# A pooled store of two tiles, sent as two transfers of the even and of the odd partitions

**Chip and metric.** One core of a Trainium2 chip. The time is device microseconds of one execution, as a median of several; before the change 3103.71 us over four runs (3103.39 to 3103.87). The experiments ran in three batches on other chips of the same kind, each with the kernel before beside it (medians 3103.55 to 3103.66 us).

## The reference

Average pooling, window 2 by 2 and step 2, over 32 x 128 planes of 256 by 256 float32:

```python
x = np.random.randn(32, 128, 256, 256).astype(np.float32)   # kernel_size 2, stride 2
for i in range(h_out):
    for j in range(w_out):
        window = x[:, :, 2*i:2*i + 2, 2*j:2*j + 2]
        output[:, :, i, j] = np.mean(window, axis=(2, 3))
```

1073.7 MB are read and 268.4 MB written, each byte once, and there is next to nothing to compute.

## The kernel before

A tile holds 32 pairs of input rows on each of 128 partitions: 64 KB a partition, 8 MB in all. Two input tiles and two result buffers exist. SyncE loads the even partitions of each tile and ScalarE's queue the odd ones, so each load is 64 partitions with a step of two. VectorE adds the two rows and then neighbouring columns, ScalarE multiplies by 0.25, and the results of two tiles lie side by side in one buffer of 32 KB a partition. GpSimd stores that buffer when both are scaled; it then waits for the store before this one and tells VectorE that that one's buffer is free.

```python
xp = xv[0:last].rearrange("(k o p t g) f -> t o k p g f", o=2, t=2, p=P // 2, g=TILE)
op = ov[0:last].rearrange("(k o p g) f -> k p o (g f)", o=2, p=P // 2, g=2 * TILE)
# ...
def load(odd, k, b):
    (act if odd else sp).dma_start(out=ins[b][odd::2], in_=xp[b, odd][k]).then_inc(loaded[b], 16)

def sums(it, dst):
    dve.tensor_add(out=it[:, :, 0:w], in0=it[:, :, 0:w], in1=it[:, :, w:]).then_inc(halfway)
    take(dve, halfway)
    dve.tensor_add(out=dst, in0=it[:, :, 0:w:2], in1=it[:, :, 1:w:2]).then_inc(summed)

def tile_sums(t):
    if t % 2 == 0:
        take(dve, emptied[t // 2 % 2])      # the result buffer is free
    take(dve, loaded[t % 2], 32)            # both halves of the tile are there
    sums(ins[t % 2], res[t % 4])
# ...
def store(k, c):
    take(pool, scaled, 2)
    pool.dma_start(out=op[k], in_=both[c].rearrange("p t g f -> p (t g f)")).then_inc(stored[c], 16)

def emptied_by(c, landed):
    pool.wait_ge(stored[c], landed)
    pool.sem_inc(emptied[c])
# ... the GpSimd program:
store(0, 0)
with pool.Fori(0, (pairs - 3) // 2) as i:
    for c in (1, 0):
        store(2 * i + (2 - c), c)
        emptied_by(1 - c, 16 * i + 16)
# ... the last pair's store is SyncE's; one tile and three pieces follow as a tail
```

Of the kernel before, what the change touches and what calls it, by code (L numbers as in the profile page):

```python
# [9 lines left out]
@with_exitstack  # L10
def kernel(
    ctx: ExitStack,
    tc: tile.TileContext,
    x: bass.AP,
    kernel_size: bass.AP,
    stride: bass.AP,
    out: bass.AP,
):
    nc = tc.nc
    P = nc.NUM_PARTITIONS  # L20

    n, c, h, w = x.shape
    k = int(kernel_size)
    s = int(stride)
    h_out = (h - k) // s + 1
    w_out = (w - k) // s + 1
    R = n * c * h_out
    units = R // P if R % P == 0 else 0


    if k == 2 and s == 2 and h % 2 == 0 and w == 256 and units >= 1024 and (units - 1) // 64 % 2 and (units - 1) // 32 % 2:
        _pool_2x2(ctx, tc, x, out, units)
    else:
        _generic_pool(ctx, tc, x, out, k, s, n, c, h, w, h_out, w_out)


TILE = 32


def _pool_2x2(ctx, tc, x, out, units):  # L40
    nc = tc.nc
    P = nc.NUM_PARTITIONS
    f32 = mybir.dt.float32
    w = x.shape[3]
    w_out = w // 2
    sp, act, dve, pool = nc.sync, nc.scalar, nc.vector, nc.gpsimd

    xv = x.rearrange("n c (ho a) w -> (n c ho) (a w)", a=2)
    ov = out.rearrange("n c ho wo -> (n c ho) wo")









    in_pool = ctx.enter_context(tc.tile_pool(name="inp", bufs=2))
    out_pool = ctx.enter_context(tc.tile_pool(name="outp", bufs=2))  # L60
    ins = [in_pool.tile([P, TILE, 2 * w], f32, name="in_tile") for _ in range(2)]
    both = [out_pool.tile([P, 2, TILE, w_out], f32, name="res") for _ in range(2)]
    res = [both[t // 2][:, t % 2] for t in range(4)]

    def sem(name):
        return ctx.enter_context(nc.semaphore(name))

    loaded, free, stored, emptied = [
        [sem(f"{n}{b}") for b in range(2)] for n in ("loaded", "free", "stored", "emptied")
    ]  # L70
    halfway, summed, scaled, held, done, tail = [
        sem(n) for n in ("halfway", "summed", "scaled", "held", "done", "tail")
    ]



    def take(engine, sem, n=1):
        engine.wait_ge(sem, n)
        engine.sem_inc(sem, -n)  # L79

    def block(r0, g):
        rows = slice(r0, r0 + g * P)
        return xv[rows].rearrange("(p g) f -> p g f", p=P), ov[rows].rearrange("(p g) f -> p g f", p=P)

    pairs, rest = divmod(units - TILE - 1, 2 * TILE)
    whole, rest = 2 * pairs + 1, rest + 1
    assert pairs % 2 and pairs >= 5 and rest <= TILE
    last = 2 * pairs * TILE * P
    xp = xv[0:last].rearrange("(k o p t g) f -> t o k p g f", o=2, t=2, p=P // 2, g=TILE)
    op = ov[0:last].rearrange("(k o p g) f -> k p o (g f)", o=2, p=P // 2, g=2 * TILE)  # L90
    parts, a = [], 0
    while a < rest:
        b = rest if rest - a <= 8 else a + (rest - a) // 2
        parts.append((a, b, sem(f"part{len(parts)}")))
        a = b

    def load(odd, k, b):
        (act if odd else sp).dma_start(out=ins[b][odd::2], in_=xp[b, odd][k]).then_inc(loaded[b], 16)

    def load_block(odd, dst, r0, g, landed):  # L100
        (act if odd else sp).dma_start(out=dst[odd::2], in_=block(r0, g)[0][odd::2]).then_inc(landed, 16)

    def load_last(odd):
        for a, b, part in parts:
            load_block(odd, ins[whole % 2][:, a:b], (whole * TILE + a) * P, b - a, part)
# [8 lines that stand above are left out]
            take(dve, emptied[t // 2 % 2])  # L114
        take(dve, loaded[t % 2], 32)
        sums(ins[t % 2], res[t % 4])

    def scale(dst, sem):
        act.mul(out=dst, in_=dst, mul=0.25).then_inc(sem)  # L119

    def next_load(b, *what):

        take(act, summed)
        act.sem_inc(free[b])
        what[0](1, *what[1:])

    def store(k, c):
        take(pool, scaled, 2)
        pool.dma_start(out=op[k], in_=both[c].rearrange("p t g f -> p (t g f)")).then_inc(stored[c], 16)  # L129

    def emptied_by(c, landed):
        pool.wait_ge(stored[c], landed)
        pool.sem_inc(emptied[c])

    with tc.tile_critical():

        for b in range(2):
            load(0, 0, b)
        with sp.Fori(1, pairs) as k:
            for b in range(2):  # L140
                take(sp, free[b])
                load(0, k, b)
        take(sp, free[0])
        load_block(0, ins[0], last, TILE, loaded[0])
        take(sp, free[1])
        load_last(0)
        take(sp, held, 2)
        c = (pairs - 1) % 2
        sp.dma_start(out=op[pairs - 1], in_=both[c].rearrange("p t g f -> p (t g f)")).then_inc(tail, 16)


        for b in range(2):
            dve.sem_inc(emptied[b])
        with dve.Fori(0, whole // 4):
            for t in range(4):
                tile_sums(t)
        for t in range(whole - whole % 4, whole):
            tile_sums(t)
        it = ins[whole % 2]
        dst = ins[(whole + 1) % 2].rearrange("p g (s f) -> p (g s) f", s=4)[:, 0:TILE]  # L160
        for a, b, part in parts:
            take(dve, part, 32)
            sums(it[:, a:b], dst[:, a:b])


        for b in range(2):
            load(1, 0, b)
        with act.Fori(0, (pairs - 1) // 2) as i:
            for c in range(2):
                for b in range(2):  # L170
                    next_load(b, load, 2 * i + (c + 1), b)
                    scale(both[c][:, b], scaled)
        c = (pairs - 1) % 2
        next_load(0, load_block, ins[0], last, TILE, loaded[0])
        scale(both[c][:, 0], held)
        next_load(1, load_last)
        scale(both[c][:, 1], held)
        take(act, summed)
        scale(res[(whole - 1) % 4], done)
        take(act, done)  # L180
        act.dma_start(out=block(last, TILE)[1], in_=res[(whole - 1) % 4]).then_inc(tail, 16)
        for a, b, _ in parts:
            take(act, summed)
            scale(dst[:, a:b], done)
            take(act, done)
            act.dma_start(out=block((whole * TILE + a) * P, b - a)[1], in_=dst[:, a:b]).then_inc(tail, 16)


        store(0, 0)
        with pool.Fori(0, (pairs - 3) // 2) as i:  # L190
            for c in (1, 0):
                store(2 * i + (2 - c), c)
                emptied_by(1 - c, 16 * i + 16)
        store(pairs - 2, 1)
        for c in range(2):
            emptied_by(c, 16 * (pairs - 1) // 2)
        pool.drain()


        take(sp, tail, 16 * (len(parts) + 2))  # L200


def _generic_pool(ctx, tc, x, out, k, s, n, c, h, w, h_out, w_out):
# [92 lines left out]
```

## Time and profile before

| | before |
|---|---|
| median of four runs | 3103.71 us |
| span of the profiled run | 3102.0 us |
| sum of all packet times, per DMA engine | 3102.1 us |
| DMA engine idle up to the last packet, mean of the sixteen | 5.1 us, all of it at the start and the end |
| VectorE idle before the row additions | 1390.8 us |

These are lines of the timeline of the kernel before for VectorE alone (start, duration, engine, line, operation; in brackets the idle time ahead of it and what ended that):

```profile
1515.20 8.69 DVE L108 TENSOR_TENSOR in_tile<-in_tile 128x8192 f32<-128x8192 f32 x1 [10.92 <-DVEq L79]
...
1540.58 8.69 DVE L108 TENSOR_TENSOR in_tile<-in_tile 128x8192 f32<-128x8192 f32 x1 [12.11 <-DVEq L79]
...
1587.73 8.69 DVE L108 TENSOR_TENSOR in_tile<-in_tile 128x8192 f32<-128x8192 f32 x1 [11.95 <-DVEq L79]
```

"DVEq L79" is the line of the helper that waits on any semaphore, so the name of the releaser does not say whether it was the load or the result buffer. The landing times do: the tile's last load semaphore came at 1515.07 for the first of these, the buffer's at 1512.46. VectorE waited for the load, here and at all 62 tiles at which it needs an earlier store to be done.

### The profile page before, as it was taken

The numbers are of one execution on the slowest core, as the hardware profiler recorded it, in microseconds if no ns is written. First come the engines' busy times: TensorE is split into PE (matmuls) and PEld (weight loads), VectorE is DVE, ScalarE is ACT, GpSimd is POOL, SyncE is SP. The second block draws the span as 40 slices with busy tenths as digits, with TensorE's granted clock in tenths as the row PEclk, the third lists the DMA queues.
The fourth block names the chain that finished last, engine by engine and source line by source line (L and its number), as shares of the span: only waits on it lengthen the run. The fifth ranks groups of instructions, "written<-read, shape, count | busy, mean of one in ns | idle before, by whom it ended". The sixth has DMA issues, their size and how long they took to land. (4 is left out here: it accounts for less than half of the span.)

```text
span 3102.0 us, 2728 instructions
## 1 busy us (share of the span) xinstructions
DVE 1679.3 (54%) x260; ACT 503.0 (16%) x161; POOL 38.0 (1%) x66
## 2 busy tenths in 40 slices
DVE  5555555555555555555555555555555555555555
ACT  1111112111111111111111111211112111121111
POOL 0000000000000000000000000000000000000000
DMA  9999999999999999999999999999999999999999
GB/s 419 433 434 437 433 433 428 438 433 432 433 440 428 434 441 433 427 433 439 432 433 438 428 438 431 434 434 432 435 436 433 439 432 433 434 431 434 434 433 406
DMA packets 30448, 1342.20 MB, mean 433 GB/s; under 512 B 5232, under 2 KB 5232, under 8 KB 5488
## 3 DMA queue, kind: packets, MB, share of 16 engines
q10 hardware_dynamic: 10976, 541.07, 40.3%
q1 hardware_dynamic: 10544, 541.07, 40.3%
q0 software_dynamic: 8928, 260.05, 19.4%
HBM read 1073.74 MB, written 268.44 MB: 433 GB/s over the span
## 5 line engine op out<-in xcount | busy, mean ns | idle before, releaser
L108 DVE TENSOR_TENSOR in_tile<-in_tile 128x8192 f32<-128x8192 f32 (+1 forms) x130 | 1112.9, 8561 | 1390.8 <-DVEq L79 1390.8
L119 ACT ACTIVATE res<-res 128x4096 f32<-128x4096 f32 x127 | 459.2, 3616 | 1967.0 <-ACTq L79 1943.3
L110 DVE TENSOR_TENSOR res<-in_tile 128x4096 f32<-128x4096 f32 x127 | 561.9, 4425 | 18.6
L119 ACT ACT_TABLE_LOAD x31 | 39.8, 1283 | 613.0 <-ACTq L79 613.0
L129 POOL DMA_DIRECT2D out_dram<-res x62 | 37.8, 610 | 2971.0 <-POOLq L79 2579.3
L119 ACT ACTIVATE in_tile<-in_tile 128x1024 f32<-128x1024 f32 (+1 forms) x3 | 4.0, 1341 | 7.3 <-ACTq L79 7.3
L110 DVE TENSOR_TENSOR in_tile<-in_tile 128x1024 f32<-128x1024 f32 (+1 forms) x3 | 4.7, 1581 | 0.4
L277 POOL MEMSET const-float32-0.0<- 128x1 f32 x1 | 0.1, 93 | 0.4 <-issue 0.4
L277 POOL MEMSET const-bfloat16-1.0<- 128x1 bf16 x1 | 0.1, 95 | 0.0
L277 POOL MEMSET const-float32-1.0<- 128x1 f32 x1 | 0.1, 93 | 0.0
L277 POOL MEMSET const-uint8-127<- 128x1 uint8 x1 | 0.1, 93 | 0.0
## 6 DMA issues: line engine op xcount, KB each, us to landing
out_dram<-res POOLq DMA_DIRECT2D x62, 4096.0 KB, 49.7
out_dram<-res SPq DMA_DIRECT2D x1, 4096.0 KB, 33.4
in_tile<-in_x_dram ACTq DMA_DIRECT2D x1, 2048.0 KB, 15.3
in_tile<-in_x_dram SPq DMA_DIRECT2D x1, 2048.0 KB, 18.1
in_tile<-in_x_dram ACTq DMA_DIRECT2D x2, 1024.0 KB, 23.0
in_tile<-in_x_dram SPq DMA_DIRECT2D x2, 1024.0 KB, 23.1
out_dram<-res ACTq DMA_DIRECT2D x1, 2048.0 KB, 16.1
in_tile<-in_x_dram ACTq DMA_DIRECT2D x127, 32.4
```

The lines of the kernel that those rows point to most:

```text
L108: dve.tensor_add(out=it[:, :, 0:w], in0=it[:, :, 0:w], in1=it[:, :, w:]).then_inc(halfway)
L110: dve.tensor_add(out=dst, in0=it[:, :, 0:w:2], in1=it[:, :, 1:w:2]).then_inc(summed)
L119: act.mul(out=dst, in_=dst, mul=0.25).then_inc(sem)
L129: pool.dma_start(out=op[k], in_=both[c].rearrange("p t g f -> p (t g f)")).then_inc(stored[c], 16)
L277: nc = _bacc.Bacc("TRN2", target_bir_lowering=False, num_devices=1)
```

## The change

Its intent, as its form suggests: stores in the shape that the loads have, each half going to a contiguous 2 MB of the output. Semaphore counts double.

```diff
-    op = ov[0:last].rearrange("(k o p g) f -> k p o (g f)", o=2, p=P // 2, g=2 * TILE)
+    op = ov[0:last].rearrange("(k o p g) f -> o k p (g f)", o=2, p=P // 2, g=2 * TILE)
...
+    def store_from(engine, k, c, landed):
+        for o in range(2):
+            src = both[c][o::2].rearrange("p t g f -> p (t g f)")
+            engine.dma_start(out=op[o][k], in_=src).then_inc(landed, 16)
+
     def store(k, c):
         take(pool, scaled, 2)
-        pool.dma_start(out=op[k], in_=both[c].rearrange("p t g f -> p (t g f)")).then_inc(stored[c], 16)
+        store_from(pool, k, c, stored[c])
...
-        sp.dma_start(out=op[pairs - 1], in_=both[c].rearrange("p t g f -> p (t g f)")).then_inc(tail, 16)
+        store_from(sp, pairs - 1, c, tail)
...
-                emptied_by(1 - c, 16 * i + 16)
+                emptied_by(1 - c, 32 * i + 32)
...
-            emptied_by(c, 16 * (pairs - 1) // 2)
+            emptied_by(c, 16 * (pairs - 1))
...
-        take(sp, tail, 16 * (len(parts) + 2))
+        take(sp, tail, 16 * (len(parts) + 3))
```

## The prediction

Its sum came to 3103.6 + 0.6 = 3104.2 us, put at 3104.5 for the tail.

> **What bounds the kernel now.** I read the page's busy slices first, then its DMA queues, then the groups and waits, and last a stretch of the timeline and the landing times in the middle of the run. The first two say almost everything:

> ```profile
> span 3102.0 us, 2728 instructions
> ...
> DVE 1679.3 (54%) x260; ACT 503.0 (16%) x161; POOL 38.0 (1%) x66
> ...
> DMA  9999999999999999999999999999999999999999
> ...
> q10 hardware_dynamic: 10976, 541.07, 40.3%
> q1 hardware_dynamic: 10544, 541.07, 40.3%
> q0 software_dynamic: 8928, 260.05, 19.4%
> HBM read 1073.74 MB, written 268.44 MB: 433 GB/s over the span
> ```

> No compute engine is busy for more than 54%, the DMA row shows 9 in all 40 slices, and the three queues' packets fill 40.3 + 40.3 + 19.4 = 100.0% of sixteen engines' span. The transfers bound this kernel; nothing is left over for a wait to occupy. The packet records give the same from below: a 64 KB load packet takes 2418 ns and a 32 KB store packet 1213 ns, nearly all of them to the nanosecond, so 27.1 GB/s for each engine and 433 GB/s for sixteen. The packet times add up to 3102.1 us for each engine. Sixteen packets are in flight at practically every moment; fewer than that for under 4 us in all, at the ends.

> The waits of the compute engines are therefore waits for the transfers, which the timeline shows:

> ```profile
> 1549.41 4.42 DVE L110 TENSOR_TENSOR res<-in_tile 128x4096 f32<-128x4096 f32 x1
> 1554.15 0.50 ACTq L98 DMA_DIRECT2D in_tile<-in_x_dram  x1
> ...
> 1559.07 0.61 POOL L129 DMA_DIRECT2D out_dram<-res  x1 [48.95 <-POOLq L79]
> 1562.52 8.69 DVE L108 TENSOR_TENSOR in_tile<-in_tile 128x8192 f32<-128x8192 f32 x1 [8.68 <-DVEq L79]
> ...
> 1576.13 0.50 ACTq L98 DMA_DIRECT2D in_tile<-in_x_dram  x1
> ...
> 1606.22 0.61 POOL L129 DMA_DIRECT2D out_dram<-res  x1 [46.54 <-POOLq L79]
> ```

> VectorE needs 8.69 + 4.42 = 13.1 us for a tile and idles 8.7 to 12.1 us before each. Two tiles, that is one store, go by in 48.4 us. The load issued at 1554.15 is followed by the landing of the tile before it at 1562.4, so 8 us of the previous load were still queued when the new one came; at the next tile (1576.13 against 1587.6) it was 11 us. The engines' queues have 8 to 11 us in hand before a late load could leave them dry.

> The store is the part to look at:

> ```profile
> out_dram<-res POOLq DMA_DIRECT2D x62, 4096.0 KB, 49.7
> out_dram<-res SPq DMA_DIRECT2D x1, 4096.0 KB, 33.4
> ```

> From issue to landing a store takes 49.7 us (last column), a little more than the period. An engine that takes one packet from each queue in turn spends 2 x 2.418 + 1.213 = 6.05 us on a round; a store is 8 packets on each engine, so 8 x 6.05 = 48.4 us. The store thus lasts as long as the tile pair it belongs to, and its buffer is needed again just after: over the run the store lands a median of 3.2 us before the load that VectorE waits for at the same tile (0.2 to 4.1 us).

> [...]

> **The change part by part.** It removes 63 store transfers of 4 MB over 128 partitions and adds 126 of 2 MB over 64 partitions with a step of two. Bytes and size of packet (32 KB) stay: 128 data packets for a pair of tiles before and after, 8 on each engine, now 4 and 4. What changes:

> Completion packets. A GpSimd store has (8928 - 7936) / 62 = 16 of them, one on each engine, of 9 ns in the packet records. There are 63 more on each engine: 63 x 9 ns = 0.57 us, all of it on the bound resource. This is the only certain cost: +0.6 us, or 0.02%.

> Issues. 62 more on GpSimd of at most 0.61 us, 38 us of an engine that is idle for 99% of the time; the landing of the previous store is acknowledged after this second issue, about 0.6 us later than now when that landing came early. In the timeline that is 1559.26 to perhaps 1560.3 against the load's landing at 1562.4: still before. One more issue on SyncE at the end (0.64 us for the last store) is in front of transfers that wait in a queue anyway. On the path: 0.

> Completion in the middle. [...]If the store queue sat out for it, the other two queues have load packets for 4.8 us in every round, so the engine stays busy. At worst the store misses one turn of 4.8 us; less the 3.2 us of slack, VectorE is 1.6 us late, with 8 to 11 us of loads in hand. On the path: 0, as long as something else is queued.

> Order of the writes. Even partitions write one half of an 8 MB block of the output, odd ones the other. Before, an engine's packets could alternate between the halves, now they go through one and then the other. The packets are at their floor of 1213 ns, so this can't gain; and loads in just this shape are at their floor, so I see nothing to lose.

> Sum: 3103.6 + 0.6 = 3104.2 us. What the tail makes of it can move the end by some us either way, more likely later since there is no idle time to win: I say 3104.5.

> **The rivals.** First, that the store's completion becomes the bound: VectorE waits for the buffer and not for its load. For it: only 3.2 us of slack, and a store as long as its period. Against it: when a store lags, loads took its turn, and the engines are no less busy. For a loss, the loads must run dry: delays above 8 us in every pair. If each of 63 pairs lost 2 us of all engines, it would be 126 us, 3230 us; I give this 1 to 2%.

> Second, that the 64-partition store from GpSimd is spread badly, over eight engines for example. For it: no such GpSimd store is in this trace. Against it: loads with the same 64 partitions have 4 packets on each of sixteen engines. If it were so, eight engines would have 38.7 + 19.4 = 58.1 us of packets in each pair instead of 48.4: 20% longer, some 3700 us. I give it 1%.

> Third, that it gains: contention between packets that the old order causes disappears, or the first half of a store starts its buffer sooner. Against it: the buffer is released only after both halves, packets are at their floor, and what is idle in the whole run is startup and tail, some 10 us. The most it could make is about 3095 us.

> **Range and chances.** The three runs before lie within 0.5 us. The certain term is 0.6 us, the tail's phase may be worth 1 to 3 us, and a small loss by queues running short for moments some us more: 3101 to 3110 holds most of it. Faster by over 2% would need 62 us that the engines do not idle: 0.5%. Slower by over 2% is the first two rivals: 2.5%. The rest, 97%, is within 2%.

> **What would show each step.** Right: GpSimd's queue has 8928 + 62 x 16 = 9920 packets and the share of the three queues still adds up to 100%; SP's queue has 16 more; GpSimd shows 124 store issues and 2048 KB each, with the second of a pair landing about 50 us after its issue and the first about 25; 32 KB packets stay at 1213 ns; VectorE's total idle time before the tile additions stays near 1391 us. Wrong: slices of the DMA row below 9 in the middle, packets of over 1213 ns, a store that lands after the load of the same tile, or VectorE idle for well above 1391 us. A change of the end by more than 10 us in either direction would make the prediction wrong, whatever its cause.

## The result

The changed kernel takes 3104.9 us (four runs, 3104.58 to 3105.97) against 3103.71. The ratio is 1.0005 with a 95% interval of 0.9987 to 1.0022: the same. Executions over 1.5% slower than the fastest of the same kernel are left out of the means. (Ratios here are the mean time of one kernel's fast runs over that of the other's fast runs of the same rounds, so not quite the ratio of the medians quoted.)

From the page of the changed kernel, its head and its DMA queues:

```profile
span 3103.3 us, 2911 instructions
...
DVE 1679.3 (54%) x260; ACT 503.0 (16%) x161; POOL 67.2 (2%) x128
...
q10 hardware_dynamic: 10976, 541.07, 40.3%
q1 hardware_dynamic: 10560, 541.07, 40.2%
q0 software_dynamic: 9920, 260.05, 19.4%
...
out_dram<-res POOLq DMA_DIRECT2D x124, 2048.0 KB, 42.0
out_dram<-res SPq DMA_DIRECT2D x2, 2048.0 KB, 32.4
```

The bytes and shares stand as they were, to 0.1%; GpSimd's queue has 992 more packets and SyncE's 16, which are the completion packets. The 42.0 us to landing is a median over both halves of the stores and the time of neither (see below). VectorE's part has changed, though. Its timeline in the same stretch:

```profile
1517.42 8.69 DVE L108 TENSOR_TENSOR in_tile<-in_tile 128x8192 f32<-128x8192 f32 x1 [13.53 <-DVEq L79]
...
1539.00 8.69 DVE L108 TENSOR_TENSOR in_tile<-in_tile 128x8192 f32<-128x8192 f32 x1 [8.32 <-DVEq L79]
...
1557.50 1.12 POOL L132 DMA_DIRECT2D out_dram<-res  x2 [47.27 <-POOLq L79]
1565.78 8.69 DVE L108 TENSOR_TENSOR in_tile<-in_tile 128x8192 f32<-128x8192 f32 x1 [13.52 <-DVEq L79]
...
1587.39 8.69 DVE L108 TENSOR_TENSOR in_tile<-in_tile 128x8192 f32<-128x8192 f32 x1 [8.34 <-DVEq L79]
```

The first tile of each pair now has 13.5 us of idle time ahead of it and the second 8.3, always. The load for the tile at 1565.78 had landed at 1563.1; the buffer's release came at 1565.54, once the last semaphore of the odd half had arrived at 1565.49. VectorE waits for the result buffer instead of the load, by 2.4 us (1.2 at the last), at 62 of these 62 tiles, where before the buffer was first by a median of 3.2 us. The waits, summed over the run (total us, times, longest), before and after:

```profile
DVE in_tile L108 <- DVEq L79: 1390.8, 127, 23.7
```

```profile
DVE in_tile L108 <- DVEq L79: 1393.3, 127, 23.6
```

So the releaser changed and the sum did not: what VectorE waits longer in one tile it waits less in the next, because the transfers set the pace.

**Where the buffer's slack went.** The packet records tell it when they are put in the order in which one DMA engine works. (The records do not name the engine; each packet was given to the engine that had just come free, which leaves no gaps.) L is a 64 KB load packet of 2.418 us, S a 32 KB store packet of 1.213 us, a dot a completion packet of 9 ns; q0 is GpSimd's queue, q1 and q10 those of SyncE and ScalarE. The changed kernel, one engine, start in us:

```
1529.17 q10:L  1531.59 q0:S  1532.80 q1:L  1535.21 q10:.  1535.22 q0:S
1536.43 q1:.   1536.43 q10:L 1538.85 q0:.  1538.85 q1:L   1541.27 q10:L
1543.68 q0:S   1544.89 q1:L  1547.31 q10:L 1549.72 q0:S
```

Counted in turns: an undivided store has 8 data packets on each engine and 1 completion, 9 turns; the divided one has 4 + 1 + 4 + 1 = 10. The loads of the two tiles have 2 x (4 + 1) = 10 turns on each of their queues. Before, the store had a turn to spare in each pair of tiles, and its landings were spaced irregularly (46.4 to 50.3 us, 5th to 95th percentile). Now it has exactly as many turns as the loads, and runs in lockstep with them: landings every 48.35 to 48.45 us, the odd half 24.2 us after the even one, each time one load packet (2.4 us) behind the load that VectorE wants. In the same window of before the dot at 1557.85 was followed by a round in which q0 had nothing, for the next store had been issued only at 1559.07.

**Where the 1.3 us of span went.** The packet times add up to 3102.80 us per engine in place of 3102.15, which is 0.65: the 63 completions of 9 ns (0.57) and less than 0.1 of scatter. The engines' mean idle time rose from 5.1 to 5.9 us, in the last hundred microseconds: VectorE's last pieces begin 2.4 us later (the last small store is issued at 3092.95 against 3090.51). Of these 2.4, 1.1 are the load of the last even tile landing later (3062.97 against 3061.90), and the rest is its buffer, released 1.3 us after that load where before the buffer was first. The two together, 0.65 + 0.86, exceed the 1.3 by 0.2, because packets overlap by some nanoseconds where one hands over to the next (7.0 us for each engine in all before, 7.2 after).

### The profile page after: what moved, and what is told of

It is laid out like the page before. It is cut to its first block, busy times and chain, and to the rows that moved or that the text cites. A ratio compares the mean times of both kernels' runs of the same rounds, so it can differ in the third digit from the quotient of the medians.

```text
span 3103.3 us, 2911 instructions
## 1 busy us (share of the span) xinstructions
DVE 1679.3 (54%) x260; ACT 503.0 (16%) x161; POOL 67.2 (2%) x128
## 2 busy tenths in 40 slices
DMA  9999999999999999999999999999999999999999
## 3 DMA queue, kind: packets, MB, share of 16 engines
q10 hardware_dynamic: 10976, 541.07, 40.3%
q1 hardware_dynamic: 10560, 541.07, 40.2%
q0 software_dynamic: 9920, 260.05, 19.4%
HBM read 1073.74 MB, written 268.44 MB: 432 GB/s over the span
## 5 line engine op out<-in xcount | busy, mean ns | idle before, releaser
L108 DVE TENSOR_TENSOR in_tile<-in_tile 128x8192 f32<-128x8192 f32 (+1 forms) x130 | 1112.9, 8561 | 1393.3 <-DVEq L79 1393.3
L110 DVE TENSOR_TENSOR res<-in_tile 128x4096 f32<-128x4096 f32 x127 | 562.0, 4425 | 18.6
L132 POOL DMA_DIRECT2D out_dram<-res x124 | 67.0, 540 | 2942.3 <-POOLq L79 2939.5
L110 DVE TENSOR_TENSOR in_tile<-in_tile 128x1024 f32<-128x1024 f32 (+1 forms) x3 | 4.7, 1580 | 0.4
## 6 DMA issues: line engine op xcount, KB each, us to landing
out_dram<-res ACTq DMA_DIRECT2D x1, 2048.0 KB, 14.2
in_tile<-in_x_dram ACTq DMA_DIRECT2D x127, 30.9
```

Of the source, the lines that this page charges most:

```text
L132: engine.dma_start(out=op[o][k], in_=src).then_inc(landed, 16)
```

## The experiments

The theory to test: **turns**. What decides is how many packets, completions included, a store has on each engine, against the 10 of the loads. Rivals: **confirmation** (a divided store costs only one more completion, called a receipt in the expectations, and one more issue; how long it would wait for a receipt no trace shows, and the landing times given for this rival were my guess), and **shape** (64 partitions in place of 128, or which 64, is what delays it). I worked expectations out by stepping through the three queues of one engine packet by packet, with the durations that the profile shows.

### Other partitions, same number of turns

```diff
-            src = both[c][o::2].rearrange("p t g f -> p (t g f)")
+            src = both[c][o * 64:o * 64 + 64].rearrange("p t g f -> p (t g f)")
```

> The changed kernel, but each store divided into partitions 0 to 63 and 64 to 127 in place of even and odd. Theory of turns (every packet, a completion packet of 9 ns too, takes a turn in the round of the three queues; a divided store has 8 + 2 = 10 turns, an undivided one 9, the loads of a pair 10 on each of their queues): nothing depends on which partitions, so 3105 us, store landing 2.4 us after the load of the same tile in every pair.[...]

Four executions took 3114.41, 3115.06, 3206.79 and 3219.96 us. The last two count as slow, at the same granted clock of 1.000; only a fast one was profiled (span 3113.4). In that profile the store lands 2.4 us after the load in every pair, as with even and odd, and in the loop its 32 KB packets take 1213 ns. So turns, not partitions, set the lockstep, and the other choice of partitions cost nothing there. The 10 us lie at the end. SyncE's last store runs there with few loads beside it, and after 3080 us its 32 KB packets take a mean of 2012 ns and up to 3367. Landing times and the last stretch of this kernel:

```profile
out_dram<-res SPq DMA_DIRECT2D x2, 2048.0 KB, 37.1
out_dram<-res ACTq DMA_DIRECT2D x1, 2048.0 KB, 22.7
```

```profile
3080.00:3113.00 33.00, 11.42 (x6) 5.70 (x4) 0.00 (x0) 1.00 0.84 263
```

The last figure of the second fence is GB/s: 263, over a stretch whose DMA engines are busy for 84% of it. In the kernel before the same end ran at 339 over 22 us and was done.

The same kernel with its last store whole again:

```diff
-        store_from(sp, pairs - 1, c, tail)
+        sp.dma_start(out=ow[pairs - 1], in_=both[c].rearrange("p t g f -> p (t g f)")).then_inc(tail, 16)
```

The expectation's first case is cut where marked, for the cause that it named and no run shows. If the 10 us are the tail's, it had 3105 us in the fast executions and no 32 KB packets above 1300 ns at the tail.

> The kernel with halves of adjacent partitions in the loop, but the last store undivided. [...]If they come from the loop: 3114 us again. If executions near 3210 us come again, the loop's stores cause them; if all lie within 2 us, the tail or chance did.

3104.88, 3104.90, 3105.56 and 3118.40 us (median 3105.23), ratio 1.0019 [0.9996, 1.0041]. Three of four are at the changed kernel's time and after 3080 us the 32 KB packets are back at 1213 ns: the 10 us were the tail's. The fourth, 13 us longer, cannot come from a divided last store, for this kernel has none; whether the two near 3210 above have the same cause is not shown. No profile of such an execution was had; what makes them slow stays open. No execution of the kernel with even and odd halves (nine, with the loop-only variant below) showed it.

### More transfers

```diff
-        for o in range(2):
-            src = both[c][o::2].rearrange("p t g f -> p (t g f)")
+        for j in range(4):
+            src = both[c][j::4].rearrange("p t g f -> p (t g f)")
```

> The changed kernel, but each store in four transfers, of every fourth partition. Theory of turns: 8 + 4 = 12 turns against the loads' 10; worked through packet by packet, the store lands about 12 us after the load of the same tile and VectorE waits for the buffer, but the loads in hand just cover it: 3106 us (1.1 us more of completion packets than with two). Theory of confirmation[...]: store landing 4 to 5 us after the load, 3106 us too. The time does not tell them apart, the landing does.

3143.0 us, ratio 1.0126 [1.0109, 1.0143]. Neither expectation had the time. The landing went with turns in kind: the store lands up to 14.2 us after the load, a median of 5.6, but not every time; in other pairs it lands 12 us before. The time divides so: of 38.8 us more span, 1.7 are completion packets, 4.2 idle DMA engines and 33 longer load packets, which my bookkeeping held at 2418 ns. Some 680 of the 15,600 in the loop took over 2660 ns, up to 3911; before it was 17. So there is a price even where the queues do not run empty. That uneven pacing of the loads is the cause is my guess, from one likeness: such lengths are also seen in the first 100 us (in the kernel before, 29 of 592 load packets: 13 at 2 to 3 us, where all engines begin to load at once, and 16 at 66 us). No run separates this cause from others.

```diff
-        for o in range(2):
-            src = both[c][o::2].rearrange("p t g f -> p (t g f)")
+        for j in range(8):
+            src = both[c][j::8].rearrange("p t g f -> p (t g f)")
```

> The changed kernel, but each store in eight transfers, of every eighth partition (one data packet and one completion packet on each engine for each). Theory of turns: 16 turns against 10; the store lands some 23 us after the load, the loads run dry while VectorE waits, the DMA engines idle about 3 us in each pair of tiles, period 51.4 us in place of 48.4: about 3290 us, 6% slower. Theory of confirmation: six more receipts and issues of 0.55 us, hidden by the loads in hand: 3108 us.

3440.89 us, ratio 1.1084 [1.1066, 1.1103]. Confirmation's 3108 is out, but turns' 3290 is also short by 150. The queue lines and VectorE's waits of this kernel:

```profile
q10 hardware_dynamic: 10976, 541.07, 37.3%
q1 hardware_dynamic: 10656, 541.07, 37.2%
q0 software_dynamic: 15872, 260.08, 22.9%
```

```profile
DVE in_tile L108 <- DVEq L79: 1722.7, 96, 34.1
```

The same 260 MB of stores now fill 22.9% of a longer span. Their packets have a mean of 1580 ns and their 90th percentile is 2487, twice the 1213. In the packet order it is seen where the loads have run dry and the store queue has the engines for itself: of the S packets that directly follow another S, half take over 2.0 us (mean 1908 ns), of those that follow a load packet 0.1% (mean 1274). No run shows why they take longer there. Against the packets' usual lengths, GpSimd's stores cost 182 us more and the packets of the other two queues, nearly all loads, 69; idle time of the engines is 89 us more, where the bookkeeping had some 186 (3 us in each of 62 pairs). That a store which is itself slow leaves fewer gaps would explain the difference, but was not tested. So this kernel alone does not prove turns: it mixes them with slow store packets.

### Turns without bytes and without division

```diff
         pool.dma_start(out=op[k], in_=both[c].rearrange("p t g f -> p (t g f)")).then_inc(stored[c], 16)
+        for j in range(3):
+            pool.dma_start(out=scr[0:16, c, j], in_=xv[0:16, 0:128]).then_inc(stored[c], 16)
...
-                emptied_by(1 - c, 16 * i + 16)
+                emptied_by(1 - c, 64 * i + 64)
```

> The kernel before, stores undivided over 128 partitions, but after each store GpSimd issues three tiny loads of 512 B on each of 16 partitions into a scratch tile (24 KB in all, one small packet and one completion packet on each engine each), which count towards the release of the store's buffer. Output stays right. Theory of turns: 8 + 1 + 3 x 2 = 15 turns against 10: the last tiny load lands about 20 us after the load of the same tile, period 51.4 us, about 3290 us, 6% slower, for 0.001 of the bytes. Theory that the shape of the divided store (half the partitions) is what delays it: like before, 3104 us. Theory of confirmation: 3106 us.

3373.71 us, ratio 1.087 [1.0852, 1.0888]: the store whole, 128 partitions, packets of 1213 ns, 1.5 MB more in the whole run, and 270 us longer. Shape and confirmation are both out by far. VectorE's timeline of this kernel, and three stretches of it (busy times of three engines, granted clock, DMA share, GB/s):

```profile
1502.08 8.69 DVE L110 TENSOR_TENSOR in_tile<-in_tile 128x8192 f32<-128x8192 f32 x1 [30.90 <-DVEq L81]
...
1515.26 8.68 DVE L110 TENSOR_TENSOR in_tile<-in_tile 128x8192 f32<-128x8192 f32 x1
...
1538.13 8.69 DVE L110 TENSOR_TENSOR in_tile<-in_tile 128x8192 f32<-128x8192 f32 x1 [9.62 <-DVEq L81]
```

```profile
1490.00:1540.00 50.00, 28.01 (x5) 8.52 (x3) 2.08 (x4) 1.00 0.91 378
1540.00:1590.00 50.00, 24.37 (x4) 7.23 (x2) 2.08 (x4) 1.00 0.97 420
1590.00:1640.00 50.00, 26.15 (x4) 8.52 (x3) 0.81 (x2) 1.00 0.86 365
```

VectorE stands for 30.9 us and then does two tiles at a run, the second with no wait: both input tiles lay there loaded, waiting for a result buffer, and with both full no load could be issued. One engine, its packets put in order as above, had nothing to do between 1510.3 and 1517.1. In every second pair the last semaphore of the buffer comes 19.7 us after the load, as the bookkeeping had it (20); in the others it comes 26 us before. Idle time of the engines is 212 us against 5, which is 207 of the 269 us of span; longer load packets are 55, the added packets some 7.

The same edit with one tiny load in place of three:

```diff
+        for j in range(1):
+            pool.dma_start(out=scr[0:16, c, j], in_=xv[0:16, 0:128]).then_inc(stored[c], 16)
```

> The kernel before with one tiny load after each store, counting towards the release of the buffer. Theory of turns: 8 + 1 + 2 = 11 turns against 10, just over the balance: the buffer comes free 5 to 10 us after the load of the same tile, the loads in hand cover it: 3106 us by bookkeeping, up to 3125 us if pauses of the loads slow their next packets as with four transfers. Theory of confirmation: 3104.5 us and a landing 1 to 2 us later than before, that is still ahead of the load.

3136.9 us, ratio 1.0108 [1.0091, 1.0125], above what I gave for the upper end. One turn too many, 11 against 10, and the buffer comes up to 9.8 us after the load (median 4.5); idle time of the engines is only 9.7 us, load packets are 26 us longer in all. Between the divided store's 10 turns and 11 there is a step, 1 us on one side and 33 on the other.

### Same division of bytes, smaller packets

```diff
-            src = both[c][o::2].rearrange("p t g f -> p (t g f)")
+            src = both[c][:, o].rearrange("p g f -> p (g f)")
```

> The changed kernel with the same number of transfers and bytes in each, but divided by tile in place of partition: all 128 partitions, packets of 16 KB. Theory of turns: 16 + 2 = 18 turns against 10, loads run dry in every second pair as with the three tiny transfers: between 3290 us (from bookkeeping with full-speed packets) and 3450 us (store with 15 turns measured 3374). Theory that two transfers of 2 MB cost what they cost whatever the packets: 3105 us.

3361.51 us, ratio 1.0832 [1.0816, 1.0849]. Two transfers of 2 MB each, as in the change, all 128 partitions, and 8% slower: 16 + 2 turns. The 16 KB packets take 611 ns throughout, so no store packet is slowed; the engines idle for 204 us and the buffer is 23.9 us late in every second pair. Load packets over their usual length are another 49 us.

### Giving the loads more turns

```diff
-        (act if odd else sp).dma_start(out=ins[b][odd::2], in_=xp[b, odd][k]).then_inc(loaded[b], 16)
+        for h in range(2):
+            gs = slice(h * TILE // 2, (h + 1) * TILE // 2)
+            (act if odd else sp).dma_start(out=ins[b][odd::2, gs], in_=xp[b, odd][k][:, gs]).then_inc(loaded[b], 16)
```

The expectation, for slow store packets, gave about 3118 + up to 180 us if those packets stay slow beside loads; the 180 are the 182 us of the run with eight transfers.

> The kernel with eight transfers for each store (3441 us), and now the loads are cut as well: each half load goes as two transfers of 32 KB packets. Theory of turns: the loads of a pair have 20 turns on each queue against 16 of the store, so the store is never late and the DMA engines never idle, although more packets are moved: 3104 + 7 x 63 x 9 ns of store completions + 252 x 9 ns of load completions + 1016 x 8 ns for halved packets = 3118 us, ten per cent faster than with whole loads. Rival: the eight transfers are slow by themselves[...]: stays near 3440 us.[...]

3148.02 us, ratio to before 1.0133 [1.011, 1.0156]. The store still goes as eight transfers; only the loads were chopped finer, and 293 of the 337 us came back: by the traces' sums, 83 are idle time of the engines and 174 store packets that are no longer slowed. This is the strongest of the tests, since more packets and more issues made the kernel faster. The store now lands before the load of the same tile in 61 of 62 pairs, by some 5 to 10 us. The waits of this kernel:

```profile
DVE in_tile L110 <- DVEq L79: 1433.7, 127, 24.8
```

VectorE still waits for the buffer at 53 of the 62 tiles, a median of 0.5 us after the load, because GpSimd passes the release on only after it has issued its next eight transfers:

```profile
1578.83 4.54 POOL L134 DMA_DIRECT2D out_dram<-res  x8 [49.23 <-issue]
1583.22 8.69 DVE L110 TENSOR_TENSOR in_tile<-in_tile 128x8192 f32<-128x8192 f32 x1 [13.21 <-DVEq L79]
```

Here the load had landed at 1578.42, the store some 8 us before that, and the release came at 1582.97. The engines hardly idle all the same (11 us), so landing ahead of the load and being released ahead of it are two things.

The remaining 44 us are 14 of added completions and halved packets, as worked out, 8 of store packets and 27 of load packets over their usual length, and 6 of idle engines, which add up to 55; packets that overlap at their handover take some 5 back, and the profiled execution had 49 us more span. With loads between the stores, the 32 KB store packets are nearly back at their usual length (a mean of 1229 ns, against 1580 before the loads were cut).

### Which part of the change costs its microsecond

Two kernels take the change apart: only SyncE's last store divided, or only the loop's.

```diff
-        sp.dma_start(out=op[pairs - 1], in_=both[c].rearrange("p t g f -> p (t g f)")).then_inc(tail, 16)
+        for o in range(2):
+            sp.dma_start(out=oq[o][pairs - 1], in_=both[c][o::2].rearrange("p t g f -> p (t g f)")).then_inc(tail, 16)
```

> The kernel before with only the last store, the one of SyncE, divided in even and odd partitions. If the changed kernel's 1.2 us come from the loop (0.6 us of completion packets, and a last tile that VectorE starts later because the divided store holds its buffer): 3103.7 us, as before. If they come from the divided last store at the tail: 3104.3 us or more.

3103.61 us (five runs, 3103.58 to 3104.11), ratio 1.0 [0.9987, 1.0014].

The other one is the changed kernel with this, the edit shown above for the adjacent halves:

```diff
-        store_from(sp, pairs - 1, c, tail)
+        sp.dma_start(out=ow[pairs - 1], in_=both[c].rearrange("p t g f -> p (t g f)")).then_inc(tail, 16)
```

> The changed kernel with the last store undivided. If the 1.2 us come from the loop: 3104.9 us, as with the whole change, and the store lands 2.4 us after the load in every pair. If half of it comes from the divided last store: 3104.3 us.

3105.41 us (five runs, 3104.61 to 3106.14), ratio 1.0007 [0.9993, 1.002], the store 2.4 us late in every pair. The loop carries the whole of the difference; the divided last store adds none. The intervals of both include 1, so for the size of it the traces' sums count, not these ratios.

| kernel | store's turns / loads' | DMA engines idle | time |
|---|---|---|---|
| before | 9 / 10 | 5 us | 3103.7 |
| even and odd halves | 10 / 10 | 6 us | 3104.9 |
| whole store + 1 tiny | 11 / 10 | 10 us | 3136.9 |
| four transfers | 12 / 10 | 9 us | 3143.0 |
| whole store + 3 tiny | 15 / 10 | 212 us | 3373.7 |
| eight transfers (slow store packets) | 16 / 10 | 94 us | 3440.9 |
| by tile, 16 KB packets | 18 / 10 | 204 us | 3361.5 |
| eight transfers, loads cut | 16 / 20 | 11 us | 3148.0 |

Ten kernels ran; all gave correct results. None beats the kernel before: its engines idle for 5 us of 3102, so there was nothing for these edits to win.

## Why the prediction was right, step by step

- **The bound.** Right. Queue shares of 100.0% before and 99.9% after, and packets at 1213 and 2418 ns in both.
- **Completion packets, +0.6 us.** Right: 992 and 16 more packets, as counted, and 0.57 of the 0.65 us by which the sums differ. "The only certain cost" was right too; the predicted 3104.5 and the measured 3104.9 differ by less than the spread of the runs.
- **The store's time.** Wrong in detail. "8 x 6.05 = 48.4 us" left out that a completion takes a turn. That it came out near 49.7 hid the omission. The count is 9 turns, of which one is the dot.
- **Completion in the middle.** This was called a turn missed "at worst", with VectorE then 1.6 us late. It is no worst case: it happens on every engine, in every pair, and VectorE is 2.4 us behind the load. That this cost no time was luck in part: the prediction did not count completions as turns, and so did not know that the change brings the store to exactly the loads' ten, where one more costs 33 us. The second half lands 56 us after the first issue, not 50, the first 32 and not 25, for the new store has to wait for the rest of the one before: that of 1557.50 was issued 8 us before the odd half ahead of it had landed (1565.49).
- **The sign that was to prove it wrong.** "A store that lands after the load of the same tile" came at 62 of 62 tiles. The prediction had also said why that need not cost anything: 8 to 11 us of loads are queued by the time. That second part holds; VectorE's idle time moved by 2.5 us of 1391. The sign was badly chosen: it marks a changed releaser, not a changed bound.
- **Order of the writes.** "8 MB block of the output" is a slip: a store writes 4 MB, each half 2 MB of it. That there was nothing to lose held: 32 KB packets stayed at 1213 ns, and none of GpSimd's is shorter in either kernel.
- **First rival.** Its mechanism came true and its cost did not, and the experiments show how near it was. It was put at 1 to 2% with a threshold of 8 us; a single turn more makes the buffer 4.5 us late in the median, and costs 33 us, chiefly through load packets that take longer and not through empty queues. The loss of all engines that this rival described is not seen at 12 turns and is at 15. What was held against it, that the engines are no less busy when a store lags, is so at 2.4 us of lag (5.9 us idle against 5.1) and not at 15 turns (212).
- **Second rival.** Sixteen engines took part, four packets each, as expected. 32 KB packets took clearly longer only where stores ran with few loads or none between them: a mean of 2012 ns at the tail of the adjacent halves, and of 1908 for those right behind another store packet in the eight transfers. Which partitions a store takes has a part in it, since the last store in even and odd halves kept to 1213 ns at the same place (1227 at most); no run shows the mechanism.
- **The tail.** "More likely later" was right by 0.86 us of idle engines; half of VectorE's 2.4 us at the end is the buffer's lag in the loop, the other half the later load.

## What to carry to other kernels

Where the transfers fill the span as here, count turns as well as bytes: packets plus one completion for each transfer, on each engine, for every queue, over one period of the loop. In these kernels a queue whose turns per period exceeded those of the others fell behind whatever its bytes, and what waited for it starved the rest at 15 turns against 10 (engines idle for 212 us, against 5). Fewer transfers and larger packets in that queue (3104.9 us with two transfers against 3143.0 with four; 3104.9 with 32 KB packets against 3361.5 with 16 KB), or smaller packets in the others (3148.0 against 3440.9), restored the balance. And a wait whose releaser has changed is not yet a loss: look whether the bound resource goes idle.
